# Delta rule: parts bound behind the filler ahead of them, keys projected ahead of z, and v scaled on VectorE

## The chip, the cores and the metric

The kernel runs on one core of a Trainium2 chip. The metric is the device time of one execution in microseconds; a kernel's time is the median over several runs. The core has five engines that work side by side, each taking its own instructions in order: TensorE (PE, matmuls; PEld are its weight loads), VectorE (DVE), ScalarE (ACT), GpSimd (POOL) and SyncE (SP), which here issues most DMAs. Matmuls write into PSUM banks, and a bank can be written again only when the engine that reads the old result has done so.

## The reference

A trunk of two layers over 1024 tokens of width 1024 in fp32. Layer 0 mixes tokens with a gated MLP and a gated DeltaNet side by side, layer 1 with differential attention; each has an MLP and a gated per-layer embedding behind it. The change is in layer 0, whose core is this:

```python
proj = hn @ w_in_e[i]
a_uv, b_qkv, b_z, b_beta, b_a = jnp.split(proj, split_at, axis=-1)
a_out = gmlp_spatial_gate(jax.nn.gelu(a_uv), ...)      # v = layer_norm(v, v_gain); u * (tril(w_s) @ v + b_s)
b_out = gated_deltanet(b_qkv, b_z, b_beta, b_a, ...)
h = h + jnp.concatenate([a_out, b_out], axis=-1) @ w_out_e[i]

# gated_deltanet: qkv = silu(causal_depthwise_conv(qkv)); q, k normalized per head
beta = sigmoid(b_beta);  g = -exp(a_log) * softplus(b_a + dt_bias)
# chunk_gated_delta_rule, per chunk and head, gc = cumsum(g)
decay = where(causal, exp(gc[:, None] - gc[None, :]), 0)
a = where(strict, (k * beta) @ k.T * decay, 0);  t_mat = a + eye
u = solve(t_mat, v * beta);  w = solve(t_mat, k * beta * exp(gc))
v_new = u - w @ state
o = (q * exp(gc)) @ state + ((q @ k.T) * decay) @ v_new
state = state * exp(gc[-1]) + (k * exp(gc[-1] - gc)).T @ v_new
o = rms_norm(o, out_gain) * silu(z)
```

## The kernel before

All of layer 0's mixing is one function, `even_mix`. Its long work is the projections (`proj_qkv`, `proj_z`, `proj_uv`): matmuls called mm in the profile, split into three fp32r products (hi and lo parts of weights and inputs), 24 of 512 columns or 48 of 256 for a block of output. They are cut into units and put out by `pump(n)`, which continues a stream until n units are out. This is the filler. The rest is the delta rule, in eight chunks of 128 tokens and four heads:

- `ahead(c)`, for each chunk before any chunk is solved: load the cumulated gates (du), 8 exps on ScalarE (L1632) with a mask by GpSimd (L1633), transposes pk of the key part, from them the inverse lengths (`inverse_length`, L1605 to L1610) and kt (L1642), small factors sc (L1646 to L1649), the products pkk = k k^T, and L1657, which multiplies pkk by sc and the exps on VectorE. am, du and kt are spilled to DRAM and the diagonal 32x32 blocks go to `diag` (L1614, L1660).
- `solve()`: one forward substitution for all diagonal blocks at once, 60 dependent instructions on VectorE (L1675, L1676), then the result is written to `solved` (L1679).
- `inverse(c)`: loads the solved blocks (L1717), transposes them (L1721) and joins them to the inverse of a whole chunk: py, copy by ScalarE (L1735), pz, copy by VectorE (L1745), and again py, L1752, pz, L1757 in size 64.
- `prep(c)`: reads v and q back by token, scales v (L1697), forms pkq. `step(c)`: the recurrence (pks, po, pvn, pst). `emit_out`: the output's norm and gate.
- `gates()` makes the gates from the last 8 columns of the first z projection; pg and pgt are its two matmul steps, and the exps need it. `norm_v` is the layer norm of the gated MLP's v half.

After each conv projection block of keys, values and queries comes an epilogue: L1420 reads PSUM into cx, three L1426 and one L1430 on VectorE with ScalarE between, and for values and queries a transpose L1382. L222 on VectorE makes the lo part of a weight from what ScalarE cast (L221).

What sets the order: a scheduler puts the instructions of each engine into one order, and the class `Ordered` ties matmuls. `behind(inst, mark)` adds an order of issue, without a semaphore, between an instruction and an earlier matmul. Filler matmuls are bound behind the delta rule's matmuls of `LAG` = 3 slots earlier; `floor` binds a delta rule matmul behind the given one; `mark` is the last matmul written. `slot()` ends a slot. FILLA, FILLB, FILLC and FILLS are the filler units given to `ahead`, the solver, the first chunk and the eight chunks. PSUM has four kinds of buffers (mm, sc, aux, tr) of two banks each; pkk lies in aux, pk in tr.

Of the kernel before, what the change touches and what calls it, by code (L numbers as in the profile page):

```python
# [13 lines left out]
AF = mybir.ActivationFunctionType  # L14
ALU = mybir.AluOpType
# [16 lines left out]
KA = (6, 5)  # L32
MARKS = ((64, 50), (192, 144), (223, 168))
TAIL = 220
FILLA, FILLB, FILLC = 40, 64, 48
IDLE = 5
FILLS = (23, 23, 23, 23, 28, 28, 28, 28)

# [76 lines left out]
class Trunk:  # L115
# [1165 lines left out]
    def even_mix(self, first, rows_of_rest, rest_of_x, w_in, ws, bs, conv, a_log, dt_bias, v_gain, o_gain, masks, w_out, gain_next, h_dram):  # L1281
# [33 lines left out]
        def bc(ap, n, ax=2):  # L1315
            sh = list(ap.shape)
            sh.insert(ax, n)
            return ap.unsqueeze(ax).to_broadcast(sh)
# [196 lines left out]
        def norm_v(hf):  # L1515

            assert len(closed) >= 4
            gv = guv[1, hf] = self.slot(("A2", "A0")[hf], [P, 4, 512], F32, "guv")
            gu = guv[0, hf] = self.slot(("A1", "A2")[hf], [P, 4, 512], F32, "guv")
            vg = self.slot("c10", [P, 512], F32, "vg")  # L1520
            nc.sync.dma_start(vg, v_gain.partition_broadcast(P))
            for t2 in range(2):
                ts = slice(2 * t2, 2 * t2 + 2)
                nc.sync.dma_start(gv[:, ts], uv_dram[1, 4 * hf + 2 * t2 : 4 * hf + 2 * t2 + 2].rearrange("t p f -> p t f"))
                mean = self.sp.tile([P, 2, G], F32, tag="lmean", name=self.nm("mean"))
                var = self.sp.tile([P, 2, G], F32, tag="lvar", name=self.nm("var"))
                for i in range(2):
                    t = 2 * t2 + i
                    x = gv[:, t].rearrange("p (g d) -> p g d", d=HD)
                    nc.vector.tensor_reduce(mean[:, i], x, AX.X, ALU.add)  # L1530
                    nc.vector.tensor_scalar(mean[:, i], mean[:, i], 1.0 / HD, None, ALU.mult)
                    nc.gpsimd.tensor_tensor(x, x, bc(mean[:, i], HD), ALU.subtract)
                    sq = self.tmp()
                    nc.scalar.activation(sq, gv[:, t], AF.Square)
                    nc.vector.tensor_reduce(var[:, i], sq.rearrange("p (g d) -> p g d", d=HD), AX.X, ALU.add)
                nc.vector.tensor_scalar(var, var, 1.0 / HD, EPS, ALU.mult, ALU.add)
                rv = self.sp.tile([P, 8], F32, tag="lrv", name=self.nm("rv"))
                nc.gpsimd.tensor_tensor(rv, flat(var), self.mhalf[:, 0:8], ALU.pow)
                for i in range(2):
                    t = 2 * t2 + i  # L1540
                    x = gv[:, t].rearrange("p (g d) -> p g d", d=HD)
                    nc.vector.tensor_tensor(x, x, bc(rv[:, 4 * i : 4 * i + 4], HD), ALU.mult)
                    nc.gpsimd.tensor_tensor(gv[:, t], gv[:, t], vg, ALU.mult)
                yield
            h1 = (256, 512)[hf]
            nc.sync.dma_start(gu[:, :, 0:h1], uv_dram[0, 4 * hf : 4 * hf + 4, :, 0:h1].rearrange("t p f -> p t f"))
# [52 lines left out]
        def part(i, c):  # L1599
            hf = c // 4  # L1600
            assert all((i, hf, m) in made for m in range(G))
            return qkv[i, hf][:, :, slice((c % 4) * P, (c % 4 + 1) * P)]

        def inverse_length(pt, name, sq):
            nc.scalar.activation(sq, pt, AF.Square)  # L1605
            l2 = self.sp.tile([P, G], F32, tag="l2", name=self.nm("l2"))
            nc.vector.tensor_reduce(l2, sq, AX.X, ALU.add)
            nc.vector.tensor_scalar(l2, l2, 4 * EPS, None, ALU.add)
            rn = self.sp.tile([P, G], F32, tag=name, name=self.nm(name), bufs=3)
            nc.gpsimd.tensor_tensor(rn, l2, self.mhalf[:, 0:G], ALU.pow)  # L1610
            return rn
# [10 lines left out]
        def ahead(c):  # L1622
# [6 lines left out]
            yield  # L1629
            for e, own, other in ((am, gsum, 1), (du, nsum, -1)):  # L1630
                for h in range(G):
                    nc.scalar.activation(e[:, h], du[:, h], AF.Exp, scale=-float(other), bias=own[:, c, h : h + 1])  # L1632
                nc.gpsimd.affine_select(e, e, pattern=[[0, G], [-other, P]], base=0, channel_multiplier=other, compare_op=ALU.is_gt if other > 0 else ALU.is_ge, fill=0.0)  # L1633
            keep(c, 1, du)

# [48 lines left out]
        def prep(c):  # L1684
            kt = fetch(c, 2, self.slot(f"c{c % 2}", [P, G, HD], F32, "kt"))
            du = fetch(c, 1, self.slot(f"c{2 + c % 2}", [P, G, P], F32, "dec"))
            home(2, c // 4)
            k, vb = part(1, c), flat(qkv[2, c // 4])[:, (c % 4) * HT : (c % 4 + 1) * HT].rearrange("p (h d) -> p h d", h=G)
            read_tokens(2, c, vb)
            if c == 0:  # L1690
                yield
            q = part(0, c)
            qt = self.slot(("d0", "c6")[c % 2], [P, G, HD], F32, "qt")
            read_tokens(0, c, qt)
            yield
            for h in range(G):
                nc.scalar.activation(vb[:, h], vb[:, h], AF.Copy, scale=hb[:, c, h : h + 1])  # L1697
            rq = inverse_length(qt, "rq", qt)
            yield
            pp = aux([P, G, P], "sc", "pkq")  # L1700
            for h in range(G):
                self.pe.matmul(pp[:, h], lhsT=k[:, h], rhs=q[:, h], start=True, stop=True)
            qk = du
            nc.vector.tensor_tensor(qk, pp, du, ALU.mult)
            mid[c] = [k, kt, vb, nbe[:, c], q, qk, rq]
            yield

        def inverse(c):
# [6 lines left out]
            for b in range(4):  # L1715
                z = slice(32 * b, 32 * b + 32)
                nc.sync.dma_start(xs[z], src[b])  # L1717
                if b < 2:
                    nc.sync.dma_start(x64[z, :, z], src[b])
            xst = inv[:, 1]  # L1720
            nc.vector.transpose(flat(xst), flat(xs))  # L1721
            xt = self.slot(f"c{4 + c % 2}", [P, G, P], F32, "xt")
            nc.gpsimd.memset(xt, 0.0)
            for b in range(4):
# [90 lines left out]
        def mixing():  # L1815
# [15 lines left out]
        states = [state]  # L1831

        fill = itertools.chain(self.stream([
            proj_qkv(1, 0, (0,)), proj_qkv(2, 0, (0,)), proj_qkv(1, 1, (0, 1)), proj_z(0),
            proj_qkv(1, 0, (1,)), proj_qkv(2, 1, (0, 1)),
            proj_uv(1, 0), proj_uv(1, 1), proj_qkv(0, 0, (0,)), proj_qkv(0, 1, (0, 1)),
            proj_z(1), proj_qkv(0, 0, (1,)), proj_qkv(2, 0, (1,)), proj_uv(0, 0), proj_uv(0, 1)], first), mixing())
        closed = []
# [23 lines left out]
        nc.vector.tensor_scalar(og, og, 0.5, None, ALU.mult)  # L1862
        for _ in rest_of_x:
            pass
        pump(96)
        gates()
        spatial_weights()
        pump(108)


        def run(g, slot=True):
# [12 lines left out]
            return [(i + 1) * n // slots - i * n // slots for i in range(slots)]  # L1884


        SLOTS = ("s", "pi", "s", "i", "p", "si", "pi")

        def chunk(st, inv, front, n, parts=SLOTS):
            gens = dict(s=st, i=inv, p=front)  # L1890
# [11 lines left out]
        solver = solve()  # L1902
        systems = [ahead(c) for c in range(NC)]
        for i, n in enumerate(share(FILLA, NC + 4)):
            for j in range(min(i, NC - 1), max(0, i - 4) - 1, -1):
                run(systems[j], False)
            self.pe.slot()
            pump(done + n)
        for n in share(FILLB, 10):
# [5 lines left out]
        invs = [inverse(c) for c in range(NC)] + [none]  # L1915
        run(invs[0], False)
        f0 = prep(0)
        chunk(none, invs[0], f0, FILLC, ("pi", "i", "i", "i", "p"))
        chunk(none, none, f0, 0, ("p", "p"))
        for c in range(NC):  # L1920
            run(invs[c + 1], False)
# [139 lines left out]
```

## Time and profile before

| | |
|---|---|
| runs | 2505.92, 2511.8, 2512.91 us |
| median of the runs | 2511.8 us |
| profiled execution, its own time | 2503.1 us |
| span of the profiled execution | 2501.4 us |
| mean granted clock of TensorE | 0.996 |
| layer 0's mixing in the span | up to about 450 us |

A row of a timeline gives the start and the duration in us, engine, line, operation, output<-inputs, shape and how many were put together; in square brackets the idle time of the engine just before, and what ended it. Line numbers are those of the kernel before. Matmuls overlap, so their pace is read from the starts of rows that follow each other, not from durations. In a row for a stretch of time the numbers are its length and the busy time of PE, PEld, DVE, ACT and POOL with their counts, then the granted clock, the share of the DMA engines and GB/s.

### The profile page before, as it was taken

The page shows a single profiled execution, that of the slowest core. Times are in us where ns is not written, and L with a number is a line of the kernel's source. Part 1 is how long each engine was busy: PE and PEld are TensorE (multiplying, and loading weights), DVE is VectorE, ACT ScalarE, POOL GpSimd, SP SyncE. Part 2 cuts the span into 40 slices and gives each one's busy share as a digit, 9 for nine tenths or more (in the row PEclk, how much of TensorE's full clock was granted, in tenths as well). Part 3 has the DMA queues.
Part 4 walks back from the last instruction along what each step waited for, and adds up shares of the span by engine and source line. Part 5 has one row for each costly group of instructions (what it writes and reads, how often), then busy time and mean ns, then how long its engine had stood idle before and what let it go on. Part 6 is the DMA issues. An engine that isn't in the chain of part 4 may idle for free.

```text
span 2501.4 us, 39807 instructions
## 1 busy us (share of the span) xinstructions
PE 2465.3 (99%) x13567; PEld 2103.8 (84%) x13567; DVE 1865.4 (75%) x3619; ACT 1290.6 (52%) x2584; POOL 314.8 (13%) x280
## 2 busy tenths in 40 slices
PE   9989999999999999999999999999999999999999
PEld 7878898888888887888899999987788888888877
DVE  7777767697667779666568878885886677788678
ACT  6643443465455444444356766664654555445543
POOL 0210242000000000000234443341000000000000
PEclk9989999999999999999999999999999999999999
DMA  7474645447555856553346776789476558657773
GB/s 246 142 202 123 166 141 182 150 146 242 174 190 206 284 175 192 187 174 118 110 110 165 158 169 162 169 241 285 133 228 197 177 181 285 220 181 205 230 230 110
DMA packets 567924, 461.96 MB, mean 185 GB/s; under 512 B 256676, under 2 KB 429736, under 8 KB 567720
## 3 DMA queue, kind: packets, MB, share of 16 engines
q1 hardware_dynamic: 533912, 455.21, 60.1%
q10 hardware_dynamic: 33808, 4.20, 1.0%
q8 instruction: 107, 1.75, 0.3%
q14 instruction: 97, 0.79, 0.1%
HBM read 322.95 MB, written 136.33 MB: 184 GB/s over the span
## 4 chain that ended last, share of the span: by engine, by line
PE 92%; DMA 3%; DVE 3%; issue 1%; SPq 1%; POOL 0%; ACT 0%; ACTq 0%; DVEq 0%; POOLq 0%
PE mm L76 81%; PE po L76 3%; PE qk L76 3%; PE aux L76 2%; PE tr L79 1%; DMA raw<-in_w_ple_gate_dram 1%; DMA raw<-in_w_mlp_dram 0%; DMA spill<-early 0%; DVE w L222 0%; PE pkq L76 0%; PE pks L76 0%; PE pgm L76 0%; PE pz L76 0%; PE py L76 0%; PE pvn L76 0%
## 5 line engine op out<-in xcount | busy, mean ns | idle before, releaser
L76 PE MATMUL mm<-g,w 128*128 128x512 f32 x2592 | 603.3, 394 | 1.0 <-DVE acc L282 0.5
L221 ACT CAST w<-raw 128x512 fp32r<-128x512 f32 x598 | 364.9, 617 | 448.2 <-PE mm L76 367.8
L76 PEld LDWEIGHTS mm<-g,w 128*128 128x128 f32 x2592 | 486.2, 188 | 115.7 <-issue 1.4
L76 PE MATMUL mm<-hi,w 128*128 128x512 f32 x1728 | 552.9, 396 | 0.3 <-ACT hi L1272 0.3
L76 PE MATMUL mm<-w,hi 128*128 128x256 f32 (+2 forms) x2528 | 504.0, 295 | 1.0 <-DVE w L222 1.0
L222 DVE TENSOR_TENSOR w<-raw,w 128x512 fp32r<-128x512 f32 x510 | 349.6, 693 | 169.9 <-ACT w L221 160.6
L76 PEld LDWEIGHTS mm<-w,hi 128*128 128x128 f32 x2528 | 402.1, 189 | 16.0 <-DVE w L222 1.2
L76 PEld LDWEIGHTS mm<-hi,w 128*128 128x128 f32 x1728 | 324.2, 188 | 73.7 <-ACT hi L1272 0.7
L76 PE MATMUL mm<-w,lo 128*128 128x256 f32 (+2 forms) x1264 | 369.0, 293 | 0.8 <-DVE lo L222 0.8
L76 PE MATMUL mm<-lo,w 128*128 128x512 f32 x864 | 341.1, 395 | 0.9 <-DVE lo L1273 0.9
L76 PE MATMUL mm<-t,w 128*128 128x512 f32 x1152 | 270.5, 394 | 1.2 <-ACT w L221 1.2
L76 PEld LDWEIGHTS mm<-t,w 128*128 128x128 f32 x1152 | 216.4, 188 | 52.1 <-ACT w L221 1.6
L76 PEld LDWEIGHTS mm<-w,lo 128*128 128x128 f32 x1264 | 238.4, 189 | 7.2 <-DVE lo L222 1.2
L76 PEld LDWEIGHTS mm<-lo,w 128*128 128x128 f32 x864 | 162.8, 188 | 37.3 <-DVE lo L1273 1.4
L222 DVE TENSOR_TENSOR g<-graw,g 128x512 fp32r<-128x512 f32 x216 | 146.8, 683 | 10.5 <-DMA gd<-g 8.2
L221 ACT CAST g<-graw 128x512 fp32r<-128x512 f32 x216 | 132.6, 617 | 41.6 <-issue 10.2
L1048 ACT ACTIVATE lg<-lg,nm 128x128 f32<-128x128 f32 (+7 forms) x128 | 99.2, 775 | 77.6 <-DVE nm L1045 76.6
L258 POOL TENSOR_TENSOR r<-ms,mhalf 128x4 f32<-128x4 f32 x12 | 12.9, 1072 | 1003.2 <-DVE ms L256 976.8
L222 POOL TENSOR_TENSOR w<-raw,w 128x512 fp32r<-128x512 f32 (+1 forms) x88 | 115.0, 1327 | 141.9 <-ACT w L221 91.8
L348 ACT ACTIVATE g<-g 128x512 f32<-128x512 f32 x96 | 60.5, 631 | 117.8 <-DVE g L282 110.8
L1045 DVE CUSTOM_DVE_ANT_0 lg<-qk,al 128x512 f32<-128x512 f32 (+3 forms) x128 | 74.6, 587 | 26.6 <-PE qk L76 21.7
L76 PE MATMUL mm<-ohi,w 128*128 128x512 f32 x256 | 85.9, 401 | 1.4 <-DVE t L1225 1.4
(332 smaller groups left out, 3518.3 us busy)
## 6 DMA issues: line engine op xcount, KB each, us to landing
raw<-in_w_mlp_dram SPq DMA_DIRECT2D x352, 256.0 KB, 3.4
graw<-gd SPq DMA_DIRECT2D x224, 256.0 KB, 2.8
gd<-g SPq DMA_DIRECT2D x192, 256.0 KB, 3.1
raw<-in_w_ple_gate_dram SPq DMA_DIRECT2D x76, 256.0 KB, 3.5
acc<-h_dram SPq DMA_DIRECT2D x64, 256.0 KB, 4.3
keep<-in_w_mlp_dram SPq DMA_DIRECT2D x64, 256.0 KB, 4.2
raw<-in_w_in_e_dram SPq DMA_DIRECT2D x60, 256.0 KB, 3.6
h_dram<-acc SPq DMA_DIRECT2D x48, 256.0 KB, 2.9
```

Of the source, the lines that this page charges most:

```text
L76: self._next(self.engine.matmul(*a, **k))
L79: self._next(self.engine.transpose(*a, **k))
L221: self.nc.scalar.copy(hi, src)
L222: (lo_engine or self.nc.vector).tensor_tensor(lo, src, f32(hi), ALU.subtract)
L258: nc.gpsimd.tensor_tensor(r, ms, self.mhalf[:, 0:4], ALU.pow)
L348: nc.scalar.activation(g, src, AF.Relu)
L1045: nc.vector.tensor_tensor_reduce(out=lg[:, k0:k1], in0=ps[:, : k1 - k0], in1=al[:, u0 + k0 : u0 + k1], scale=-1.0, scalar=3.0e38 if c == 0 ...
L1048: nc.scalar.activation(lg[:, :n], lg[:, :n], AF.Exp, bias=nm[:, r, nch - 1 : nch], scale=-1.0, accum_out=me.sums[:, b, r : r + 1])
```

## The change

Five parts, all within layer 0's mixing; from about 447 us of the profile of before on, each engine's order of instructions is the same in both kernels.

1. The second half of the first key projection stands ahead of z in the stream of filler, not behind it. The fills are 112 and 116 units (were 96 and 108), FILLA and FILLB 36 and 60 (were 40 and 64), the same sum of 260. `gates()` runs at a raised priority.
2. In the loop over `ahead`, `floor` is set to the last matmul written, so that a slot's pk and pkk come behind the filler that is written ahead of them.
3. `late(inst)` binds an instruction of another engine behind the last matmul written: the exps, v's scaling, the square for q's length, and the transpose of the solved blocks. Three of these four read what a DMA brought.
4. `inverse` has one more yield, between its loads and the transpose; two lists of slots have one more i.
5. `norm_v`: for each of 8 tiles one VectorE multiply (128x512, L1542) and one GpSimd multiply by the gain (L1543) become four VectorE operations of 128x128 that do both.

```diff
-FILLA, FILLB, FILLC = 40, 64, 48
+FILLA, FILLB, FILLC = 36, 60, 48
...
-                    nc.vector.tensor_tensor(x, x, bc(rv[:, 4 * i : 4 * i + 4], HD), ALU.mult)
-                    nc.gpsimd.tensor_tensor(gv[:, t], gv[:, t], vg, ALU.mult)
+                    for h in range(G):
+                        nc.vector.scalar_tensor_tensor(x[:, h], x[:, h], rv[:, 4 * i + h : 4 * i + h + 1], vg[:, h * HD : (h + 1) * HD], ALU.mult, ALU.mult)
...
+        def late(inst):
+            self.pe.behind(inst, self.pe.mark)
+
         def inverse_length(pt, name, sq):
-            nc.scalar.activation(sq, pt, AF.Square)
+            inst = nc.scalar.activation(sq, pt, AF.Square)
+            if name == "rq":
+                late(inst)
...
-                    nc.scalar.activation(e[:, h], du[:, h], AF.Exp, scale=-float(other), bias=own[:, c, h : h + 1])
+                    late(nc.scalar.activation(e[:, h], du[:, h], AF.Exp, scale=-float(other), bias=own[:, c, h : h + 1]))
...
-                nc.scalar.activation(vb[:, h], vb[:, h], AF.Copy, scale=hb[:, c, h : h + 1])
+                late(nc.scalar.activation(vb[:, h], vb[:, h], AF.Copy, scale=hb[:, c, h : h + 1]))
...
+            yield
             xst = inv[:, 1]
-            nc.vector.transpose(flat(xst), flat(xs))
+            late(nc.vector.transpose(flat(xst), flat(xs)))
...
-            proj_qkv(1, 0, (0,)), proj_qkv(2, 0, (0,)), proj_qkv(1, 1, (0, 1)), proj_z(0),
-            proj_qkv(1, 0, (1,)), proj_qkv(2, 1, (0, 1)),
+            proj_qkv(1, 0, (0,)), proj_qkv(2, 0, (0,)), proj_qkv(1, 1, (0, 1)), proj_qkv(1, 0, (1,)),
+            proj_z(0), proj_qkv(2, 1, (0, 1)),
...
-        pump(96)
-        gates()
+        pump(112)
+        with self.tc.high_priority(EARLY):
+            gates()
         spatial_weights()
-        pump(108)
+        pump(116)
...
-        SLOTS = ("s", "pi", "s", "i", "p", "si", "pi")
+        SLOTS = ("si", "pi", "s", "i", "p", "si", "pi")
...
+            self.pe.floor = self.pe.mark
             for j in range(min(i, NC - 1), max(0, i - 4) - 1, -1):
                 run(systems[j], False)
+            self.pe.floor = None
             self.pe.slot()
...
-        chunk(none, invs[0], f0, FILLC, ("pi", "i", "i", "i", "p"))
+        chunk(none, invs[0], f0, FILLC, ("pi", "i", "i", "i", "ip"))
```

In the changed kernel the lines from 1605 on are 3 to 6 higher: the exps are L1637, L1657 is L1662, the solver L1680 and L1681, L1697 is L1702, L1721 is L1727, L1752 is L1758.

What this does to the order is shown at three places. The first is TensorE where the last two chunks are put ahead (pk transposes and pkk products; mm is filler). Before:

```order
L76 MATMUL mm_1742<-w_1628,lo_188 128x256
L76 MATMUL mm_1742<-w_1628,hi_199 128x256
L76 MATMUL mm_1742<-w_1629,hi_199 128x256
L76 MATMUL mm_1742<-w_1628,lo_200 128x256
L79 MATMUL pk_1566<-ident,qkv_701 128x128 x4
L79 MATMUL pk_1646<-ident,qkv_701 128x128 x4
L76 MATMUL pkk_1689<-qkv_701 128x128 x4
L76 MATMUL mm_1742<-w_1191,hi_127 128x256
```

With the change, where pkk_1681 is that of chunk 5 and pk_1661 the transposes of chunk 7:

```order
L76 MATMUL pkk_1627<-qkv_699 128x128 x4
L76 MATMUL mm_1714<-w_1240,hi_145 128x256
L76 MATMUL pkk_1681<-qkv_699 128x128 x4
L76 MATMUL mm_1714<-w_1239,lo_146 128x256
L76 MATMUL mm_1714<-w_1239,hi_154 128x256
L76 MATMUL mm_1714<-w_1240,hi_154 128x256
L76 MATMUL mm_1714<-w_1239,lo_155 128x256
L76 MATMUL mm_1714<-w_1398,hi_163 128x256
L79 MATMUL pk_1661<-ident,qkv_699 128x128 x4
```

The last chunks' transposes and products stood one behind the other before; now filler stands between them, and behind pkk_1681 come 41 filler matmuls before pkk of chunk 6 and 36 more before that of chunk 7.

The second place is VectorE at the end of the solver. Before, its last steps stand ahead of L1420 of mm_2281:

```order
L222 TENSOR_TENSOR w_2341<-raw_2338,w_2340 128x512
L1676 TENSOR_TENSOR work_1773<-work_1773,outer_1777 128x2x29
L1675 TENSOR_TENSOR outer_1777<-work_1773 128x30
L1676 TENSOR_TENSOR work_1773<-work_1773,outer_1777 128x30
L1420 TENSOR_TENSOR cx_2353<-mm_2281,rb_224 128x512
L1422 COPY carved_240<-cx_2353 128x3
```

With the change they stand behind L1420 of mm_2424, two blocks of 24 matmuls later:

```order
L1420 TENSOR_TENSOR cx_2471<-mm_2424,rb_224 128x512
L1426 SCALAR_TENSOR_TENSOR t_2411<-cx_2407,cols,t_2411 128x512
L1680 TENSOR_TENSOR outer_1805<-work_1801 128x58
L1422 COPY carved_240<-cx_2471 128x3
L1419 MEMSET cx_2519 128x3
L1681 TENSOR_TENSOR work_1801<-work_1801,outer_1805 128x2x29
L1680 TENSOR_TENSOR outer_1805<-work_1801 128x30
L1681 TENSOR_TENSOR work_1801<-work_1801,outer_1805 128x30
```

The transpose of the first chunk's solved blocks (L1727) moved with them, and L1420 of the next block is ahead of it too:

```order
L1420 TENSOR_TENSOR cx_2519<-mm_2488,rb_224 128x512
L1422 COPY carved_240<-cx_2519 128x3
L1430 SCALAR_TENSOR_TENSOR qkv_2279<-t_2480,t_2475 128x512
L1426 SCALAR_TENSOR_TENSOR t_2523<-cx_2519,cols,t_2523 128x512
L1382 STREAM_TRANSPOSE t_2480<-qkv_2279 128x512
L1426 SCALAR_TENSOR_TENSOR t_2523<-cx_2519,cols,t_2523 128x512
L1727 STREAM_TRANSPOSE inv_2303<-inv_2303 128x128
```

On TensorE the py of this chunk, which needs that transpose, comes right behind the 24 matmuls of mm_2488 and the first pkq and pks.

The third place is ScalarE in the middle of the recurrence. Before, three chunks' scaling of v (L1697) stands together ahead of the copy L1752, which pz needs:

```order
L1799 ACTIVATE qkv_274<-qkv_2279 128x4x128
L1499 ACTIVATE t_3690<-mm_3563,r_217 128x256 x2
L1697 ACTIVATE qkv_3645<-qkv_3645,carved_240 128x128 x12
L1752 COPY inv_3593<-py_3808 64x256
L1809 ACTIVATE qkv_2279<-qkv_2279,fo_3878 128x128 x4
L1697 ACTIVATE qkv_3645<-qkv_3645,carved_240 128x128 x4
```

With the change four of them stand behind that copy and the others in their own chunks:

```order
L1805 ACTIVATE qkv_274<-qkv_2279 128x4x128
L1499 ACTIVATE t_3690<-mm_3563,r_217 128x256 x2
L1758 COPY inv_3593<-py_3808 64x256
L1815 ACTIVATE qkv_2279<-qkv_2279,fo_3878 128x128 x4
L1702 ACTIVATE qkv_3645<-qkv_3645,carved_240 128x128 x4
```

## The prediction

> **What bounds the kernel now.** I read the page first, for the engine that is busy nearly all the time.
>
> ```profile
> PE 2465.3 (99%) x13567; PEld 2103.8 (84%) x13567; DVE 1865.4 (75%) x3619; ACT 1290.6 (52%) x2584; POOL 314.8 (13%) x280
> ```
>
> TensorE is idle for 2501.4 − 2465.3 = 36.1 us in all. The change adds and removes no matmul, so it can gain no more than these 36 us plus what matmuls lose at a reduced clock. Hence I took TensorE's waits in 60 to 460 us, the stretch that the change reorders.
>
> ```profile
> PE pkk L76 <- DVE early L1657: 8.8, 1, 8.8
> PE mm L76 <- DVE alo L1580: 2.2, 1, 2.2
> PE pz L76 <- issue: 2.2, 1, 2.2
> PE pk L79 <- DVE kt L1642: 1.5, 2, 1.0
> PE mm L76 <- DVE w L222: 1.0, 1, 1.0
> ```
>
> These are total us, times, longest. Three places hold nearly everything: 131 to 149 us (pkk, pk and one w: 8.8 + 1.5 + 1.0 = 11.4 us), 322 us (pz) and 387 us (alo). Their timeline and the busy time of PE, PEld, DVE, ACT, POOL by 10 us, with the granted clock behind:
>
> ```profile
> 144.75 2.07 PE L76 MATMUL pkk<-qkv 128*128 128x128 f32 x8 [8.83 <-DVE early L1657]
> 147.27 0.63 PE L76 MATMUL mm<-w,hi 128*128 128x256 f32 x2
> 147.91 0.63 PE L76 MATMUL mm<-w,hi 128*128 128x256 f32 x2
> 149.66 1.05 PE L76 MATMUL pkk<-qkv 128*128 128x128 f32 x8
> 150.47 0.48 PE L76 MATMUL mm<-w,hi 128*128 128x256 f32 x2
> 150.90 0.40 PE L76 MATMUL mm<-w,hi 128*128 128x256 f32 x2
> 151.26 0.40 PE L76 MATMUL mm<-w,hi 128*128 128x256 f32 x2
> 130.00:140.00 10.00, 3.35 (x20) 2.31 (x18) 9.71 (x21) 8.14 (x21) 5.03 (x6) 0.75 0.99 279
> 140.00:150.00 10.00, 5.25 (x30) 5.25 (x31) 10.00 (x39) 1.24 (x2) 2.94 (x3) 0.57 0.72 186
> 320.00:330.00 10.00, 7.82 (x70) 7.58 (x69) 3.10 (x8) 8.05 (x25) 2.91 (x4) 1.00 0.57 182
> 380.00:390.00 10.00, 7.80 (x71) 6.08 (x71) 9.92 (x15) 2.58 (x5) 7.41 (x6) 1.00 0.70 221
> ```
>
> The reader is to see two things. Around 140 us VectorE is full (9.71 and 10.00 of 10), so the wait is for a queue of VectorE work and not for one late instruction. And the clock was 0.75 and 0.57 there, but 1.00 around the two waits of 2.2 us. What the low clock cost: a group of three matmuls took 147.91 − 147.27 = 0.64 us against 151.26 − 150.90 = 0.36, and the eight pkk until the next matmul 146.5 − 144.75 = 1.7 against 150.47 − 149.66 = 0.8. That is 0.9 + some 1.0 for the three groups up to 148.6 + some 0.4 for the pk ahead, about 2.3 us. The first place is worth 11.4 + 2.3 = 13.7 us, all three 18.1.
>
> **The first place.** The second last pkk waits for its PSUM bank, which the L1657 of 143.58 frees. The order rows show pk, pk and pkk of the last chunks with no filler between them before; now 41 and 36 filler matmuls stand ahead of the last two pkk, at 0.12 us each 4.9 and 4.3 us, and the epilogues of two key blocks, five rows of 0.7 us each on VectorE, went ahead of z. But z now pushes the gates back: the transposed gates (pgt) come behind some 8 us more of matmuls, by counting rows up to it, and the exps can't start before them.
>
> ```profile
> 101.72 0.27 PE L79 MATMUL pgt<-ident,carved 128*32 128x128 f32 x1
> 143.58 1.12 DVE L1657 SCALAR_TENSOR_TENSOR early<-pkk,sc,early 128x128 f32<-128x128 f32 x4
> 150.75 1.13 DVE L1657 SCALAR_TENSOR_TENSOR early<-pkk,sc,early 128x128 f32<-128x128 f32 x4
> 107.09 7.14 ACT L1632 ACTIVATE early<-early,carved 128x128 f32<-128x128 f32 x24 [3.91 <-DVE sc L1646]
> ```
>
> So pgt comes at 110 instead of 101.72, and the exps near 116 instead of 107.09. Adding up VectorE's new queue from the gates (110 us) to the L1662 that frees the bank for the last pkk, at 0.7 us for a row of 512 columns, 0.28 for one of the four of an L1657 and 0.1 for a small one, gives 29 us, thus 139; TensorE is there at 140. Level, but ACT can be the later one. I leave 2.5 us of waiting, with ends of 0 (VectorE in time) and 6 (exps a further 4 us behind); waits of 2.2 us cost no clock above. **Term: −13.7 + 2.5 = −11.2.**
>
> **The new wait, the solver.** Before, the solver's last steps stood ahead of the epilogue of mm_2281. Now its tail stands behind L1420 of mm_2424, two column blocks later, and VectorE takes its instructions in order. What follows the last step has rows:
>
> ```profile
> 192.94 0.19 DVE L1676 TENSOR_TENSOR work<-work,outer 128x30 f32<-128x30 f32 x1
> 193.43 0.47 SPq L1679 DMA_DIRECT2D solved<-work  x1
> 197.21 0.69 DVE L1420 TENSOR_TENSOR cx<-mm,rb 128x512 f32<-128x512 f32 x1 [4.08 <-PE mm L76]
> 198.18 0.33 SPq L1717 DMA_DIRECT2D inv<-solved  x1
> 202.26 0.31 DVE L1721 STREAM_TRANSPOSE inv<-inv 128x128 f32<-128x128 f32 x1 [0.94 <-DMA inv<-solved]
> 198.41 0.62 PE L76 MATMUL mm<-hi,w 128*128 128x512 f32 x2
> 199.11 0.63 PE L76 MATMUL mm<-hi,w 128*128 128x512 f32 x2
> 206.16 0.44 PE L76 MATMUL py<-inv,am 32*32 32x32 f32 x16
> ```
>
> From the solver's end (193.13) to the transpose it took 9.1 us, through one write, one load and their waits, and py ran at 206.16 with no idle time before it. In the new order, count from the end of mm_2424: L1420 0.7, L1426 0.7 and four solver steps of 0.2 with two small copies make 2.4 us, then 9.1, then the transpose 0.3: py can start at 11.8. TensorE meanwhile has 24 matmuls of mm_2488 (three in 199.11 − 198.41 = 0.70, so 5.6) and seven of pkq and pks (0.2 each by the eight records of pkk in 0.8), together 7.1. It then waits 4.7; I take 5. The lower end doesn't need the DMAs: L1727 also stands behind L1420 of mm_2488 and five rows of 0.7, which gives 10.6 and a wait of 3.5. The upper end, 6, adds a slower load. A wait of 5 us lies between the 2.2 that cost no clock and the 8.8 that cost 2.3; I put 1.0 on it. **Term: +6.0** (3.5 to 8.3).
>
> [...]
>
> **The wait at 322 us.** ScalarE stood in v's scaling, which had waited for a DMA, with the copy that pz needs behind it:
>
> ```profile
> 320.21 3.62 ACT L1697 ACTIVATE qkv<-qkv,carved 128x128 f32<-128x128 f32 x12 [3.91 <-DMA qkv<-by_token]
> 323.74 0.34 ACT L1752 COPY inv<-py 64x256 f32<-64x256 f32 x1
> ```
>
> Three chunks' scaling stood there, hoisted. Bound behind TensorE, each chunk's four go to their own place, and L1758 of this chunk now stands ahead of the next L1702. **Term: −2.2** (0 if another chunk's scaling takes the place).
>
> **The wait at 387 us.** VectorE again, with two of its instructions stretched while GpSimd multiplied by the gain:
>
> ```profile
> 380.15 1.29 DVE L1542 TENSOR_TENSOR guv<-guv,rv 128x512 f32<-128x512 f32 x2
> 382.80 2.38 DVE L1542 TENSOR_TENSOR guv<-guv,rv 128x512 f32<-128x512 f32 x2
> 385.10 3.42 DVE L222 TENSOR_TENSOR w<-raw,w 128x512 fp32r<-128x512 f32 x2
> 384.72 3.25 POOL L1543 TENSOR_TENSOR guv<-guv,vg 128x512 f32<-128x512 f32 x2 [0.69 <-DVE guv L1542]
> ```
>
> An undisturbed pair takes 1.29, so GpSimd cost VectorE 1.1 + 2.1 = 3.2 us here. The change drops those eight GpSimd rows and gives VectorE four operations a tile at 0.28 (the L1657 row) in place of one at 0.65: +0.5 a tile, +1.9 for four tiles. Net −1.3, but L1775 of one chunk (four of 0.28) now comes ahead of alo as well. I take −0.4, with ends of −2.2 (the whole wait) and +1.9 (no relief). The other four tiles lie where TensorE does not wait; without that cover they would cost 1.9 more. **Term: −0.4.**
>
> [...]
>
> The fill counts (108 + 152 before, 116 + 144 now), the floor and the extra yield carry no instruction of their own: their effect is the order above. Nothing changes in order behind 447 us, so nothing there is costed.
>
> **Sum.** −11.2 + 6.0 − 2.2 − 0.4 = −7.8 us against the profiled execution: 2503.1 − 7.8 = 2495.3. That execution is 8.7 below the median of the runs (2511.8); taking the same distance, the predicted median is 2511.8 − 7.8 = 2504.0.
>
> **The rivals.**
>
> *All three places close, and the solver's tail is covered after all.* Speaks for it: py had slack before. Against: mm_2424 must end before the tail can run, whatever the speed of VectorE. −13.7 − 2.2 − 1.3 = −17.2, so 2494.6. Chance 0.15.
>
> *The wait only moves.* The exps start 9 us later; if ACT, 8.14 of 10 busy at 130 to 140, holds the last pkk back by 6 us, and py's wait costs its upper 8.3: −7.7 + 8.3 − 2.2 − 0.4 = −2.0, so 2509.8. For it: VectorE's 139 against TensorE's 140 is no margin. Against: the pk and pkk that waited stood without filler between them, and no longer do. Chance 0.22.
>
> *Scaling in place blocks each chunk.* In its own place v's scaling (L1702) stands just ahead of L1758 in at least three of the seven later chunks. If its load lands late there as it did at 320 us, each chunk pays the 2.2 us of pz: from four chunks on the gain is gone (7.8 / 2.2 = 3.5), with all seven it is −7.8 + 15.4 = +7.6, so 2519.4, slower. Against: the load is issued one step ahead of the scaling, and the binding puts TensorE work between them. Chance 0.18.
>
> That the change does not do what it says is excluded by the order rows; how much VectorE needs is not.
>
> **How the numbers follow.** The forecast has 0.45, its own range 2500 to 2508 from the ends of its first two terms. About 7.5 us (0.3%) is what a measurement of this kernel can tell from no change, so the forecast lies on that border and goes half and a little more to faster. Faster: 0.15 + 0.28 = 0.43 and a little of the second rival, 0.45. Slower: most of the third, with a little for other late work of this kind, 0.18. Same: the rest, 0.37. The range 2494 to 2515 holds the first two rivals and half of the third.
>
> **What would show it.** Right: pkk's wait under 4 us and clock 1.00 at 130 to 150; a new wait of py of 3.5 to 6 us near 190, behind DVE L1727; no pz wait at 322; L222 pairs at 1.3 and alo's wait under 2.2. Wrong: pkk still waiting 6 us or more, py without a wait, pz waits in several chunks behind L1702, or alo's wait grown.

## The result and the profile after

| | before | changed | ratio of the runs, 95% interval |
|---|---|---|---|
| first measurement, median of 20 runs each | 2505.82 us | 2503.53 us | 0.9984 (0.9976 to 0.9992) |
| again, 33 and 11 runs | 2506.46 us | 2498.42 us | 0.9971 (0.9962 to 0.9980) |
| profiled executions, span | 2501.4 us | 2505.9 and 2497.0 us | |

By the ratios, which compare means, the change makes the kernel faster by 4.0 us (2.0 to 6.0; the medians differ by 2.3), in the second measurement by 7.3 us (5.0 to 9.5); 7.8 were forecast. One run of f4 below, 4069.1 us at a granted clock of 0.555 where every other run has 0.993 or more, is left out of its ratio. The profiled execution of the changed kernel in the first measurement took 2507.6 us, among the longest of its 20 runs (2496.5 to 2507.8 us), and shows a longer span than that of before. So the span is the wrong thing to compare here. What the change touches ends at a place that both kernels share, the first pab that waits for ScalarE's rb. I call its start the stage end. Before, and with the change (timeline of TensorE: start, duration, row, idle time before it and what ended it):

```profile
453.92 0.66 PE L79 MATMUL pab<-ident,qkv 128*128 128x128 f32 x4 [0.24 <-ACT rb L265]
```

```profile
451.02 0.66 PE L79 MATMUL pab<-ident,qkv 128*128 128x128 f32 x4 [0.24 <-ACT rb L265]
```

The stage became 2.9 us shorter; what follows, in the same order of instructions, took 2047.5 us before and 2054.9 after. Over all 14 profiled executions of this study that rest scatters from 2047.0 to 2054.9 us. A second profile of the changed kernel (r1 below) has its stage end at 447.12, 6.8 us earlier than before, and a rest of 2049.9. So the two ratios and the two stage ends tell one story: some 3 to 7 us gained, in the stage.

TensorE's waits in the first profile of the changed kernel, 60 to 460 us (total us, times, longest):

```profile
PE mm L76 <- ACT t L1499: 2.5, 1, 2.5
PE pvn L76 <- DVE xt L1763: 2.5, 1, 2.5
PE py L76 <- issue: 1.8, 1, 1.8
PE pkq L76 <- DVE qkv L1430: 1.4, 1, 1.4
PE pkk L76 <- DVE early L1662: 0.7, 2, 0.5
```

None of the large waits of before is in this list: pkk has 0.7 us in place of 8.8, pk, pz and the alo of 387 us are gone. Four others stand there instead. Where they lie, with the rows of ScalarE and VectorE just ahead of them:

```profile
143.38 5.91 ACTq L1385 DMA_DIRECT2D by_token<-t  x4
149.41 0.63 ACT L1428 ACTIVATE t<-t 128x512 f32<-128x512 f32 x1 [6.67 <-DMA by_token<-t]
152.09 2.03 ACTq L1385 DMA_DIRECT2D by_token<-t  x4
154.32 0.63 ACT L1428 ACTIVATE t<-t 128x512 f32<-128x512 f32 x1 [3.67 <-DMA by_token<-t]
157.16 0.54 PE L76 MATMUL mm<-w,hi 128*128 128x256 f32 x2 [2.50 <-ACT t L1499]
206.54 0.49 PE L76 MATMUL pkq<-qkv,qkv 128*128 128x128 f32 x2 [1.36 <-DVE qkv L1430]
208.46 0.30 DVE L1727 STREAM_TRANSPOSE inv<-inv 128x128 f32<-128x128 f32 x1
208.87 0.64 PE L76 MATMUL py<-inv,am 32*32 32x32 f32 x16 [1.84 <-issue]
380.38 2.18 DVE L1543 SCALAR_TENSOR_TENSOR guv<-guv,rv,vg 128x128 f32<-128x128 f32 x8
383.07 0.41 DVE L1763 COPY xt<-pz 64x256 f32<-64x256 f32 x1
383.54 2.08 PE L76 MATMUL pvn<-qkv,xt 128*128 128x128 f32 x8 [2.47 <-DVE xt L1763]
```

Each is a queue in order. At 157 us it is ScalarE's: it issues eight DMAs of by_token (ACTq, L1385) from its own queue, the first four spread over 5.91 us, and each tanh L1428 starts only 0.12 and 0.20 us after the issues ahead of it end; the read of a PSUM bank (L1499) that mm waits for stands behind them. At 208 py waits for the transpose L1727, which had no idle time of its own (no bracket), so VectorE's queue and not the load was last. At 383 eight operations of `norm_v` stand ahead of the copy L1763 that pvn needs. The busy time by 10 us (PE, PEld, DVE, ACT, POOL, then the granted clock, DMA share, GB/s):

```profile
150.00:160.00 10.00, 7.50 (x54) 7.29 (x53) 6.22 (x10) 5.16 (x10) 0.00 (x0) 0.87 0.88 234
160.00:170.00 10.00, 10.00 (x84) 10.00 (x83) 7.59 (x25) 3.42 (x8) 0.00 (x0) 0.96 1.07 352
200.00:210.00 10.00, 6.80 (x48) 5.62 (x47) 8.76 (x20) 2.38 (x5) 0.19 (x1) 0.93 0.45 104
210.00:220.00 10.00, 10.00 (x63) 7.88 (x62) 4.88 (x11) 2.47 (x6) 0.00 (x0) 0.90 0.31 64
380.00:390.00 10.00, 7.53 (x30) 6.53 (x31) 6.09 (x20) 1.17 (x2) 1.20 (x2) 0.66 0.74 237
```

Three stretches now have a low clock; before there was one, and most of that fell into the idle time itself. A low clock behind a wait of 2.5 us costs work: the eight pvn of 383.54 took 2.08 us, against 1.16 in r1, where the clock fell only after them, behind the same wait of 2.48 us.

### The profile page after: what moved, and what is told of

The parts are those of the page before. It is cut to its first block, busy times and chain, and to the rows that moved or that the text cites. A ratio compares the mean times of both kernels' runs of the same rounds, so it can differ in the third digit from the quotient of the medians.

```text
span 2505.9 us, 39836 instructions
## 1 busy us (share of the span) xinstructions
PE 2472.7 (99%) x13567; PEld 2109.4 (84%) x13567; DVE 1866.3 (74%) x3643; ACT 1289.0 (51%) x2584; POOL 301.9 (12%) x272
## 3 DMA queue, kind: packets, MB, share of 16 engines
q8 instruction: 107, 1.75, 0.3%
## 4 chain that ended last, share of the span: by engine, by line
PE 89%; DMA 4%; DVE 4%; issue 1%; SPq 1%; ACT 1%; POOL 0%; ACTq 0%; DVEq 0%; POOLq 0%
PE mm L76 78%; PE po L76 3%; PE qk L76 3%; PE aux L76 2%; DMA raw<-in_w_ple_gate_dram 1%; PE tr L79 1%; DMA raw<-in_w_mlp_dram 0%; DVE w L222 0%; DMA spill<-early 0%; DMA guv<-uv_dram 0%; PE pvn L76 0%; PE aux L79 0%; PE pkq L76 0%; PE pks L76 0%; PE py L76 0%
## 5 line engine op out<-in xcount | busy, mean ns | idle before, releaser
L222 DVE TENSOR_TENSOR w<-raw,w 128x512 fp32r<-128x512 f32 (+1 forms) x510 | 349.0, 691 | 172.8 <-ACT w L221 162.5
L222 DVE TENSOR_TENSOR g<-graw,g 128x512 fp32r<-128x512 f32 x216 | 147.5, 687 | 10.4 <-DMA gd<-g 7.2
L222 POOL TENSOR_TENSOR w<-raw,w 128x512 fp32r<-128x512 f32 (+1 forms) x88 | 115.5, 1332 | 142.6 <-ACT w L221 93.5
```

The costliest lines, as they stand in the source:

```text
L222: (lo_engine or self.nc.vector).tensor_tensor(lo, src, f32(hi), ALU.subtract)
```

## The experiments

All are told by the waits of TensorE in the stage and by the stage end, since these repeat better than the whole time; the ratios to the kernel before are given with 95% intervals. From r1 on, each ratio is to 14 to 33 runs of the kernel before, measured along with 4 to 11 of the variant. r1 to e3 were run on one chip, e4 to e7 on another, f1 to f4 on a third, so between these groups stage ends and waits are the better measure.

| run | pk, pkk, w near 140 | near 157 | pkq + py | pz | alo, pvn | stage end | ratio (interval) |
|---|---|---|---|---|---|---|---|
| before | 11.4 | 0 | 0 | 2.2 | 2.2 | 453.9 | 1 |
| change, first profile | 0.7 | 2.5 | 3.2 | 0 | 2.5 | 451.0 | 0.9984 (0.9976 to 0.9992) |
| r1_again | 0.2 | 1.0 | 3.2 | 0 | 2.5 | 447.1 | 0.9971 (0.9962 to 0.9980) |
| e1_norm_back | 0.2 | 0 | 3.2 | 0 | 4.0 | 448.6 | 0.9975 (0.9967 to 0.9984) |
| e2_norm_only | 11.5 | 0 | 0 | 2.6 | 0.6 | 454.4 | 0.9990 (0.9981 to 0.9998) |
| e3_order_back | 7.8 | 0 | 0 | 0 | 2.5 | 450.1 | 0.9983 (0.9974 to 0.9991) |
| e4_lag4 | 0.7 | 2.5 | 0 | 0 | 2.5 | 446.5 | 0.9954 (0.9939 to 0.9969) |
| e5_yield_tile | 0.6 | 0.8 | 3.2 | 0 | 0.5 | 444.3 | 0.9951 (0.9935 to 0.9966) |
| e6_no_late | 0.7 | 1.8 | 2.5 | 0.6 | 2.0 | 448.1 | 0.9975 (0.9965 to 0.9985) |
| e7_no_floor | 0.7 | 2.3 | 5.3 | 0 | 0.6 | 446.9 | 0.9967 (0.9954 to 0.9980) |
| f1_lag4_tile | 0.6 | 2.2 | 0 | 0 | 0.5 | 442.5 | 0.9948 (0.9935 to 0.9960) |
| f2_th_slot | 0.4 | 3.4 | 0 | 0 | 0 | 443.2 | 0.9937 (0.9923 to 0.9950) |
| f3_order_only | 0.8 | 2.7 | 8.1 | 0.9 | 1.9 | 455.0 | 0.9998 (0.9990 to 1.0007) |
| f4_no_yield | 0.2 | 0.3 | 7.2 | 0 | 2.4 | 450.3 | 0.9983 (0.9974 to 0.9992) |

Waits under 0.4 us each of other matmuls are left out, and so are three single ones: 2.1 us of mm for a weight at 172 in e2, 1.2 of po at 199 in f3, 1.7 of pkq at 307 in f2; e4 and f1 have 0.9 and 0.8 us of the next chunk's py at 231.

**The change again (r1_again).** No edit.

> The changed kernel once more, unchanged, to see what repeats. The stage end is read as the start of the first pab that waits for ACT rb (451.0 us in the first profile of it, 453.9 in that of before). Theory A (three new waits of 2 to 3 us, each with a stretch of low clock, ate the gain): the waits at 157 (mm behind ACT L1499), 206 to 209 (pkq and py) and 383 (pvn behind L1763) come again within 0.7 us each, stage end 450 to 452. Rival B (these waits are accidents of one execution, and the stage is some 8 us shorter in most): at least one of them is gone and the stage ends under 448. The rest of the program behind the stage (2054.9 us then, 2047.5 before) has the same order, so it should scatter by several us and not stay at 2055.

```profile
154.79 0.51 PE L76 MATMUL mm<-w,hi 128*128 128x256 f32 x2 [0.99 <-ACT t L1499]
202.66 0.49 PE L76 MATMUL pkq<-qkv,qkv 128*128 128x128 f32 x2 [1.36 <-DVE qkv L1430]
204.99 0.64 PE L76 MATMUL py<-inv,am 32*32 32x32 f32 x16 [1.84 <-issue]
380.87 1.16 PE L76 MATMUL pvn<-qkv,xt 128*128 128x128 f32 x8 [2.48 <-DVE xt L1763]
```

Three waits are the same to 0.01 us: they are set by the order of the queues. The one near 155 was 2.5 and is 1.0 (and 0 in e1, whose order is the same there). It goes with how long ScalarE stood idle around its first four DMA issues: 6.67 us ahead of L1428 in the first profile, 5.23 here and 4.31 in e1, while the second idle time is 3.67 us in all three. Stage end 447.1, neither as theory A nor as B had it: two of the three places are fixed, one differs from execution to execution.

**norm_v undone, and norm_v alone (e1, e2).**

```diff
-for h in range(G):
-    nc.vector.scalar_tensor_tensor(x[:, h], x[:, h], rv[...], vg[...], ALU.mult, ALU.mult)
+nc.vector.tensor_tensor(x, x, bc(rv[:, 4 * i : 4 * i + 4], HD), ALU.mult)
+nc.gpsimd.tensor_tensor(gv[:, t], gv[:, t], vg, ALU.mult)
```

> The change without its norm_v part (the gain is multiplied by GpSimd again). Theory A: VectorE's eight operations of 0.27 us no longer stand ahead of L1763, so the pvn wait of 2.5 us and the low clock at 380 to 390 (0.66) go; a wait for alo of about 2 us with clock 1.00 takes their place; stage end 1 to 2.5 us earlier than with the change, median 0.9990 to 0.9996 of the changed kernel. Rival C (contention with GpSimd is the worse evil): alo waits 2.5 us or more, the pvn wait stays, stage end equal or up to 2 us later.

> The kernel before with only the norm_v part. Theory A: the rest of the stage stays (pkk wait 8 to 9 us, pz wait 2.2), the alo wait goes or turns into a wait of 1.5 to 3 us elsewhere at 380 to 392; stage end 452.5 to 455.5, time within 0.1% of before. Rival C: stage end 451 to 452, as the 2.2 us are simply gained.

In e1, and below it in e2, the row of the wait for alo:

```profile
381.23 0.79 PE L76 MATMUL mm<-alo,w 128*128 128x512 f32 x1 [4.04 <-DVE alo L1580]
```

```profile
389.44 0.50 PE L76 MATMUL mm<-alo,w 128*128 128x512 f32 x1 [0.56 <-DVE alo L1580]
```

Theory A's number for e1 failed: pvn's wait went, but the wait for alo is 4.0 us and the clock fell to 0.66 there as well. Beside GpSimd's multiplies VectorE's work again took longer: one L222 took 1.75 us at 377.70 and 0.68 us at 388.14, where GpSimd is idle (before, two of them took 3.42 us at 385.10, beside L1543, and 1.29 at 378.36). The edit is worth 1.5 us of waiting in either surrounding (4.0 to 2.5, 2.2 to 0.6). Rival C has the better of it, but not in full: it had pvn's wait stay in e1, and e2's stage end did not come early, as a wait of 2.1 us for a weight, which no other run has there, came at 172 us.

**The projections' order undone, and alone (e3, f3).** The edit is the first part of the change: the stream's order, fills, FILLA, FILLB and the gates' priority.

> The change without its first part: z ahead of the second half of the first keys, fills and gates as before; floor, late, the extra yield and norm_v stay. Theory A: the solver's tail stands one block earlier (behind L1420 of mm_2281 instead of mm_2424), so py and pkq wait 0 to 1 us together; pvn keeps its 2.5 us. The floor alone spreads pk and pkk: pkk waits 0 to 4 us; stage end 446 to 451. Rival D (the keys ahead of z are what closed the first place): pkk waits 5 us or more with clock under 0.9 at 130 to 150, stage end 452 or later.

> The kernel before with only the first part (keys ahead of z, fills, gates at raised priority). Theory A (the order of the projections alone closed the first place): pkk waits 0 to 2 us, clock 1.00 at 130 to 150, pz near 320 and alo near 387 wait 1.5 to 4 us as before, py 1 to 4 us, since the solver's tail stands behind two more blocks; stage end 446 to 451. Rival L (it needs floor and late as well): pk and pkk wait 4 us or more, stage end 451 or later.

```profile
140.20 2.07 PE L76 MATMUL pkk<-qkv 128*128 128x128 f32 x8 [7.12 <-DVE early L1662]
```

```profile
208.76 0.64 PE L76 MATMUL py<-inv,am 32*32 32x32 f32 x16 [7.83 <-issue]
```

The first row is of e3: with z ahead of the keys again, floor, late and yield do not keep pkk from waiting 7.1 us, and py doesn't wait at all. The second is of f3: with keys ahead of z and nothing else, pkk's wait is gone and py waits 7.8 us with the clock at 0.57 and 0.75 (200 to 220 us). The time is that of before (0.9998). So rival D was right on pkk, though the stage end of 450.1 is below its bound, and theory A on f3's first place, not on py, which waits longer than it had, nor on the stage end, 455.0 against at most 451. The first part closes the first place and moves a wait of about the same size to the solver; which of its pieces does it (the order of the projections, the fills or the gates' priority) was not taken apart. Alone it gains nothing that can be told. With the others it does: without it they end the stage at 450.1 (0.9983), with it at 447.1 (0.9971, r1 on the same chip; the intervals just overlap).

**Floor, late and the extra yield undone (e7, e6, f4).**

```diff
-            self.pe.floor = self.pe.mark
             for j in range(min(i, NC - 1), max(0, i - 4) - 1, -1):
                 run(systems[j], False)
```

> The change without the floor in the loop over ahead. Keys stay ahead of z. Theory A (keys ahead of z closed the first place, and the floor does little): pkk waits 0 to 2 us, stage end within 2 us of the change's 447.1 to 451.0. Rival H (the floor closed it): pk or pkk waits 4 us or more with clock under 0.9 at 130 to 150, stage end 452 or later.

```diff
         def late(inst):
-            self.pe.behind(inst, self.pe.mark)
+            pass
```

> The change without the four bindings of late (exps, v's scaling, q's square, the transpose). The order puts twelve scalings of v ahead of L1758 again. Theory A: the pz wait near 320 us comes back with 1.5 to 3 us, the first place and py stay as with the change (pkk under 1, pkq and py 2.5 to 4.5); stage end 1 to 4 us later. Rival G (the scaling was late by its load alone, and that is earlier now): no pz wait, stage end equal within 1 us.

```diff
-            yield
             xst = inv[:, 1]
...
-        SLOTS = ("si", "pi", "s", "i", "p", "si", "pi")
+        SLOTS = ("s", "pi", "s", "i", "p", "si", "pi")
...
-        chunk(none, invs[0], f0, FILLC, ("pi", "i", "i", "i", "ip"))
+        chunk(none, invs[0], f0, FILLC, ("pi", "i", "i", "i", "p"))
```

> The change without the extra yield and with the old slot lists. VectorE's solver tail then stands ahead of L1420 of mm_2440, py is 27 rows earlier in TensorE's order. Theory A (py's wait is the distance between the solver's tail and py): py waits 3 to 9 us, more than with the yield (3.2 with pkq); stage end 0 to 6 us later than the change. Rival M (the yield is what made py late): py waits under 2 us, stage end equal or earlier.

In f4 (first fence) and e6 (second) the rows that decide:

```profile
202.75 0.64 PE L76 MATMUL py<-inv,am 32*32 32x32 f32 x16 [5.45 <-issue]
```

```profile
317.66 0.65 PE L76 MATMUL pz<-inv 64*64 64x64 f32 x8 [0.60 <-issue]
```

What py waits for differs. In the change the transpose L1727 had no idle time, so VectorE's queue set it; in f4 (first row) and f3 (second) the same transpose waited for the load of the solved blocks:

```profile
202.33 0.31 DVE L1726 STREAM_TRANSPOSE inv<-inv 128x128 f32<-128x128 f32 x1 [4.84 <-DMA inv<-solved]
208.35 0.31 DVE L1721 STREAM_TRANSPOSE inv<-inv 128x128 f32<-128x128 f32 x1 [7.14 <-DMA inv<-solved]
```

Rival H fell: without the floor pkk doesn't wait, but pkq and py wait 5.3 instead of 3.2 us, so the floor only shifts later places, and in time (0.9967) e7 can't be told from the change. Theory A held for the yield: without it pkq and py wait 7.2 us. Late: pz's wait comes back with 0.6, under either bound of theory A and above rival G's zero; twelve scalings stand ahead of L1758 again, but their load was issued 6.0 us earlier than before (310.05 against 316.04), while pz was due only 4.9 us earlier. What moved the load was not separated. In e6 the times (0.9975) and the stage end (448.1) can't be told from those of the change, so nothing here shows a gain from late.

**The two new waits cured (e4, e5, f1).** e4 binds the filler of the first chunk's slots behind the slot four before, so that more of it comes ahead of py; e5 cuts `norm_v` after each tile; f1 has both.

```diff
+        self.pe.lag = 4
         chunk(none, invs[0], f0, FILLC, ("pi", "i", "i", "i", "ip"))
+        self.pe.lag = LAG
         chunk(none, none, f0, 0, ("p", "p"))
```

```diff
                     for h in range(G):
                         nc.vector.scalar_tensor_tensor(x[:, h], ..., ALU.mult, ALU.mult)
-                yield
+                    yield
```

> The change, with the filler of the first chunk's slots bound behind the slot four before instead of three: some 31 filler matmuls (7 us) come ahead of py, and VectorE's order stays the same up to the transpose. Theory A (py waits because filler is bound behind it while the solver's tail is late): the waits of pkq and py (1.36 and 1.84 us in all three executions so far) both go, clock 1.00 at 200 to 220, pvn's 2.5 us stays, stage end 3 to 6 us before the change's 447.1 to 451.0. Rival E (the wait only moves to the next delta rule matmul, since py, pz and the second py are a chain): 2 us or more of waiting between 200 and 240 remain, stage end within 2 us.

> The change with norm_v cut after each tile instead of after each two, so that one tile's four operations (1.1 us) and no more lie between, and the last tile's four stand behind L1763. Theory A (pvn waits for L1763 because eight operations of norm_v stand ahead of it): the pvn wait of 2.5 us falls under 0.8 and alo does not wait more than 0.8; stage end 1.5 to 4 us earlier than the change. Rival F (VectorE is simply full there, whichever comes first): 2 us or more of waiting for alo or pvn at 370 to 392 remain.

> The change with both cures: first chunk's filler bound four slots back, norm_v cut after each tile. Theory A (the waits are separate terms and add): pkq and py wait under 1.2 us together, pvn and alo under 1 us, the wait for ACT L1499 near 156 stays with 0 to 2.5 us; stage end 441 to 446 (444.3 and 446.5 with one cure each), ratio to before 0.993 to 0.9955. Rival I (each cure only uncovers the next wait): stage end not under 444, ratio not under 0.9955.

Of e4 the row of the next py that waits, of e5 the row of alo:

```profile
231.70 0.44 PE L76 MATMUL py<-inv,am 32*32 32x32 f32 x16 [0.94 <-PE pvn L76]
```

```profile
379.47 0.50 PE L76 MATMUL mm<-alo,w 128*128 128x512 f32 x1 [0.54 <-DVE alo L1580]
```

Both cures did to their waits what theory A said: in e4 the 3.2 us at 207 are gone and 0.9 us come in the next chunk, in e5 the 2.5 us of pvn become 0.5 of alo, with the clock at 1.00 from 370 to 400. The stage end of e4, 446.5, is 4.5 us before that of the change's first profile, as theory A had it, but only 0.6 before that of r1: the wait near 157 was 2.5 us in this execution, as in the first profile, and the clock was low behind it (0.91 and 0.92) and behind pvn (0.83). Together (f1) they reach a stage end of 442.5, 11.4 us before that of the kernel before, and 0.9948 of its time. Rival I fell on the stage end; on the ratio the interval (0.9935 to 0.9960) takes in both sides.

**The wait near 157 (f2).** f2 is f1 with this edit:

```diff
-                        th = self.tmp()
+                        th = self.slot(("B", "c8")[ml], [P, HT], F32, "th") if (i, j, hf) == (2, 1, 1) else self.tmp()
```

> The same, and the tanh tiles of the last two value blocks lie in two free buffers of their own instead of among the four temporaries, so that L1428 does not wait for the DMAs that read an older one. Theory J (the wait near 156 is ScalarE standing in L1428 for by_token's DMAs, ahead of L1499): L1428 waits under 1 us for DMA, mm's wait for L1499 goes (under 0.4 us), clock 1.00 at 150 to 170; stage end 0 to 3 us before the kernel with both cures. Rival K (VectorE or the table load sets L1499): the wait stays at 1 to 2.5 us.

```profile
153.35 6.53 ACTq L1385 DMA_DIRECT2D by_token<-th  x8
159.92 0.62 ACT L221 CAST w<-raw 128x512 fp32r<-128x512 f32 x1 [6.83 <-DMA by_token<-th]
```

L1428 no longer waits, as theory J had it, and neither it nor rival K had the rest right: the wait for L1499 fell to 0.2 us, yet TensorE waits 2.9 us for a weight that ScalarE casts at 159.92, after eight DMA issues had been spread over 6.5 us of its queue. The clock is 0.83 at 160 to 170, and the stage ends 0.7 us after that of f1. The wait moved by one kind of instruction. So it is ScalarE's DMA issues at this place and not one buffer. Why they take so long is not shown; the DMA engines are 83% busy at 150 to 160 us. The cure is open. f2 has the best time of all, 2491.2 us and 0.9937 (0.9923 to 0.9950), but it can't be told from f1 by these runs.

## Why the prediction came out as it did

The direction and the three places hold: 7.8 us were forecast, 4.0 and 7.3 measured. That the predicted time, 2504.0 us, lies 0.5 us from the measured median of 2503.53 is luck: it was counted from 2511.8, the median of three runs, which twenty runs put at 2505.82.

Term by term the account comes out of the two profiles of the change. A term is here the change of the listed waits, plus half the time for which TensorE was busy at a clock of 0.50: 4.8 us of such time at the first place before; in the first profile 3.4 near 157, 3.2 at the solver and 6.0 behind pvn; in r1 6.5 at the solver and 3.4 behind pvn.

| term, us | forecast | first profile | r1 |
|---|---|---|---|
| first place | −11.2 | −13.1 | −13.6 |
| solver | +6.0 | +4.8 | +6.4 |
| pz | −2.2 | −2.2 | −2.2 |
| alo, with pvn | −0.4 | +3.3 | +2.0 |
| near 157 | none | +4.2 | +1.0 |
| sum | −7.8 | −3.0 | −6.4 |
| stage end | | −2.9 | −6.8 |

- *First place.* Better than forecast: pkk waits 0.2 to 0.7 us instead of 2.5, at full clock. The chain is as counted: pgt at 109.00 us (110 forecast), the exps from 114.64 (116), the bank free at 140.70 (139) and the last pkk at 140.75 (140). That the first part of the change does this, and not the filler between pk and pkk, the prediction did not separate; e7 and e3 show it: without the floor no wait of pkk, without the first part 7.1 us.
- *The solver.* The mechanism is as told: the tail stands behind L1420 of mm_2424, and py waits for the transpose. Its wait was 3.2 us (pkq 1.36, py 1.84) in place of 5. The step that was mis-sized is the path through the DMAs: 9.1 us before from the solver's end to the transpose, while with the change the write alone let the first load go 2.6 us behind its issue (200.52 to 203.12) and not 4.75. So the lower end of the term, which needs VectorE's order alone (3.5), was the right one. The clock behind it fell in every run with this wait (0.57 to 0.93 at 200 to 210 us) and in the two profiles of the change cost 1.6 and 3.2 us, where 1.0 was put on it. That the whole term still comes out near 6.0 is luck: the wait was taken too long and the clock too cheap.
- *pz.* It is gone. The reason given, scaling in its own place, is only part of it: without the bindings (e6) 0.6 us come back, not 2.2.
- *alo.* This is the term that failed. The wait for alo went and pvn's came, 2.5 us, behind the eight operations of `norm_v`, with a low clock behind it. The relief from GpSimd is as told (a pair of L222 takes 1.28 us in e2, and at 372.69 in the first profile of the change, 3.42 before), but the count of VectorE's queue was put down to alo alone; the other reader of that queue, L1763, was not looked for. e1 shows what it would have been without this part: a wait of 4.0 us.
- *What was missed:* the wait near 157 us, 0 to 2.7 us from run to run, for which no term stood. It comes with ScalarE's DMA issues, whose length differs between executions of the same order; before, e2 and e3, which keep z first, do not have it. And the clock: one long wait became three short ones, and the clock that fell behind them slowed work instead of idle time. The prediction took from the profile of before that a wait of 2.2 us costs no clock; that was the luck of where those waits lay (last section).

Of the rivals, the third (scaling in place blocks each chunk) is refuted: no pz waits at all with the change. The first (all three places close) is what f1 comes near, with two further edits. The second (the wait only moves) is what the first part does by itself: in f3 pkq and py wait 8.1 us and the time is that of before, though the last pkk is not held back as that rival had it.

## What to carry to other kernels

When an edit moves a stall on the engine that is always busy, follow the queue of the engine that released it: the next wait stands where that queue's tail was pushed. Count both the queue and the DMAs behind it, as the later one sets the wait: here it was the queue with the change and the load in f3 and f4, and the DMA path timed in the kernel before was too long. Price each new wait also by the clock behind it (1.6 and 3.2 us at the solver), and look for every reader of a crowded queue, not only for the one that waited before. And where one part of a stage changes in a long program, compare that part's end in several profiled executions, as the rest scatters by more than the gain.

## What the hardware showed

Read in fine slices, the granted clock between 60 and 460 us is 1.00 or 0.50 in all 14 executions, and it stays at 0.50 for one to four times 3.41 us: 13.65 us before (from 135.00); 3.41, 3.41 and 6.83 in the first profile of the change (from 157.48, 208.68 and 382.76); 6.83 and 3.41 in r1 (from 204.66 and 382.15). Within an execution the starts lie whole multiples of 3.41 us apart (208.68 − 157.48 is 15 of them, 382.76 − 208.68 is 51). So in these executions the clock changes only at the borders of pieces of 3.41 us. Their grid lies elsewhere in each of the three: the first starts, 135.00, 157.48 and 204.66 us, are 6.6 and 13.8 pieces apart.

Whether a piece is slow goes with how long TensorE was idle in the piece ahead of it. Three pieces of r1, around the wait of 2.48 us for pvn, then two of before, around the wait of 2.20 us for alo (the second number is the length, the third the busy time of PE, the third from the end the clock):

```profile
378.74:382.15 3.41, 1.28 (x10) 1.24 (x11) 3.35 (x10) 0.35 (x2) 0.57 (x1) 1.00 0.58 133
382.15:385.56 3.41, 3.41 (x13) 2.94 (x12) 1.19 (x5) 0.51 (x1) 0.43 (x1) 0.50 0.98 286
385.56:388.98 3.42, 3.42 (x28) 3.25 (x28) 3.04 (x8) 1.85 (x3) 0.00 (x0) 1.00 0.40 144
384.17:387.59 3.42, 2.81 (x26) 1.90 (x24) 3.42 (x4) 1.66 (x4) 2.87 (x2) 1.00 0.50 177
387.59:391.00 3.41, 1.82 (x9) 1.56 (x10) 2.55 (x5) 0.63 (x1) 0.52 (x2) 1.00 0.80 251
```

In r1 2.13 us of idle time lie in one piece, and the next is at 0.50. In before a border cuts the wait into 0.61 and 1.59 us, and the clock stays. Over all 14 executions a full-speed piece with 1.76 us or more of idle time was followed by a slow one each time (25 of them), and one with 1.68 us or less never, so the limit seen here lies between these two. So what a wait cost went with where the borders fell: those of 2.18 us (cut into 0.73 and 1.45) and 2.20 us (before) cost no clock, nor did one of 2.55 us (pz in e2), while one of 1.98 us in e6 cost a piece. The same 2.5 us of pvn cost two pieces in the first profile, where 0.78 us of them fell into the slow piece from 382.76, and one in r1, where none did. In that slow piece the 0.78 us, less than in any full-speed piece ahead of a slow one, were enough for the next to be slow as well.

Waits set by the order of queues repeat to 0.01 us in the first profile, r1 and on a further chip in e5 or e4 (1.36, 1.84 and 2.47 to 2.48), while the one behind ScalarE's DMA issues ranges from 0 to 2.5 us with the same order.
